# A transformer layer on one core: the four norm vectors brought onto all partitions by DMA instead of by TensorE

## The chip, the cores and the metric

The kernel runs on one core of a Trainium2 chip. The metric is device time in microseconds of a whole execution; less is better. The core's engines are named as in the profile: PE is TensorE's matmul side, PEld its weight loads, DVE is VectorE, ACT is ScalarE, POOL is GpSimd, SP is SyncE, which here only issues DMAs. Each engine works its own list of instructions in order and waits on semaphores for the others.

## The reference

One layer on 512 tokens of width 2048, all in float32: an input projection, three token mixers, an output projection, a first norm, a mixture of experts, a second norm. What matters here is the last part:

```python
x = layer_norm(DEEPNORM_ALPHA * x + mix, ln1_g[l], ln1_b[l])
ffn = hierarchical_moe(x, ...)      # 32 experts, 2 per token; each row is weighted by its gate
x = layer_norm(DEEPNORM_ALPHA * x + ffn, ln2_g[l], ln2_b[l])
# layer_norm(x, g, b) = (x - mu) * rsqrt(var + 1e-5) * g + b, over the 2048 columns
```

`DEEPNORM_ALPHA` is 2 ** 0.25. The gains and offsets `ln1_g`, `ln1_b`, `ln2_g`, `ln2_b` are vectors of 2048 numbers (8 KB). Tokens lie on the 128 partitions, so each vector has to stand on every partition, as a tile of 128 x 2048 (1 MB), before an engine can multiply it into token rows.

## The kernel before

All matrix products are made of three float32r products each (`mm3`, lines 138 to 141): the high parts, and high by low both ways. So each weight chunk of 128 x 1024 float32 (512 KB) is first split into two parts, the high one by ACT (line 85), the low one by DVE (line 86). `Ring` does this for the whole stream of chunks in a fixed order: SP loads a chunk as soon as a raw buffer is free (line 74), ACT and DVE split it when a pair of split buffers is free, PE uses it and gives the pair back (`done`). The raw buffers are filled far ahead of the splits. All weight DMAs leave from SP's one queue, in the order of the program.

The experts are a loop over `e` = 0 to 31. `up(e)` takes 16 chunks, makes the gate and up products of expert e, and ends with the product of the two on DVE (line 1362, tile `B`, once per expert: a good mark of the loop's pace). Behind it `down(e - 1)` takes 8 chunks and makes the rows of the expert before, which POOL adds to the DRAM accumulators `yd` by indirect DMAs (`scatter`, line 1310). POOL also gathers the token rows of expert e + 2 (`gather`, line 1295). The order of every engine's instructions is the order in which the code writes them.

Between `up(e)` and `down(e - 1)` the loop has a place for side work. With e = 12 and e = 21 SP loads two vectors each (`ln1_g` and `ln1_b`, then `ln2_g` and `ln2_b`) onto one partition of tiles `X7` and `B2` (line 1508). With e = 13 and e = 22 `spread` brings them onto all partitions: PE multiplies a row of ones with 512 columns of the vector (line 1344, four times for each tile, in plain float32), and ACT copies the product from PSUM back over the tile (line 1345), for the first norm with ALPHA as its scale. With e = 13 to 20 POOL multiplies half of a token block `z[b]` by `gb1[0]` and adds `gb1[1]` (lines 1515 and 1516), so that behind expert 20 `z` holds ALPHA times the first norm's result. The code that follows the loop adds the experts' sums to `z` and makes the second norm from `gb1` as loaded with e = 21, with EPS in `root` and `refine`.

The weight of an expert's row, `gate`, is made before the loop from `gval` and `w0`; line 1245 is the step of it that the change touches.

Of the kernel before, what the change touches and what calls it, by code (L numbers as in the profile page):

```python
# [20 lines left out]
P = 128  # L21
# [6 lines left out]
# order of the experts: one of each group in turn, so that a token's experts never lie in the same four  # L28
# [3 lines left out]
ALPHA = 2.0 ** 0.25  # L32
SCALE = 192 ** -0.5
# [11 lines left out]
class Ring:  # L45
    """Weight chunks of [128, 1024] float32, loaded ahead and split exactly into two float32r parts."""

    def __init__(self, nc, chunks, beside):
        # beside: chunks of column tiles [k, 64] whose two parts lie next to each other by tiles
        self.nc, self.chunks, self.beside = nc, chunks, beside  # L50
        self.raw, self.hl = [], []
        self.raw_of, self.hl_of = {}, {}
        self.raw_free, self.hl_free = [], []
        self.n_dma = self.n_split = self.n_use = 0
# [63 lines left out]
def _build(tc, nc, ctx, I, out):  # L118
# [28 lines left out]
    # ---------------------------------------------------------------- weight stream  # L147
# [14 lines left out]
    def carver(t):  # L162
        """Parts of a tile, one after another."""
        used = [0]

        def carve(*shape):
            n = int(np.prod(shape))
            v = t[:, used[0]:used[0] + n]
            used[0] += n
            assert used[0] <= t.shape[1]  # L170
            if len(shape) > 1:
                names = "abc"[:len(shape)]
                v = v.rearrange(f"p ({' '.join(names)}) -> p {' '.join(names)}", **dict(zip(names, shape)))
            return v
        return carve

    # what is of no use behind the attention
# [4 lines left out]
    def warm(o, n):  # L182
        """Products that keep TensorE's clock up where it has to wait."""
        for _ in range(n):
            mm(o[:, 0:256], still[:, 0:P], still, start=True, stop=True)

    # ---------------------------------------------------------------- x, split
# [23 lines left out]
    # ---------------------------------------------------------------- constants  # L211
# [19 lines left out]
    eps_c = const("eps_c", [P, 1])  # L231
# [7 lines left out]
    # the first chunk's parts in turn with those of x  # L239
# [9 lines left out]
    # small inputs  # L249
# [21 lines left out]
    # lower bounds: softmax over the layers, cumulative, less the first layer's  # L271
# [13 lines left out]
    # ---------------------------------------------------------------- phase A: x @ w_in  # L285
# [69 lines left out]
    def rotary():  # L355
        for _ in range(5):
            yield
        tt(wsT, wsT, causal[:, None, :].to_broadcast([P, 4, P]), op=OP.mult)
        # rotary tables, by tokens
        posf = early(NB)  # L360
        nc.vector.tensor_copy(posf, posi)
        ang = ftmp[:, 0:128].rearrange("p (b d) -> p b d", b=NB)
        kk_ = ftmp[:, 128:256].rearrange("p (b d) -> p b d", b=NB)
        for b in range(NB):
            ts(ang[:, b, :], invf, posf[:, b:b + 1], None, op0=OP.mult)
        ts(kk_, ang, 1.0 / (2.0 * np.pi), None, op0=OP.mult)
        ts(kk_, kk_, 12582912.0, None, op0=OP.add)
        ts(kk_, kk_, 12582912.0, None, op0=OP.subtract)
        for c in TWO_PI:
            stt(ang, kk_, -c, ang, op0=OP.mult, op1=OP.add)  # L370
        ts(kk_, ang, PI, -PI, op0=OP.min, op1=OP.max)
        act(sinT, kk_, AF.Sin)
        ts(kk_, ang, np.pi / 2, None, op0=OP.is_gt)
        ts(ang, ang, np.pi / 2, None, op0=OP.add)
        stt(ang, kk_, -2.0 * np.pi, ang, op0=OP.mult, op1=OP.add)
        ts(ang, ang, PI, -PI, op0=OP.min, op1=OP.max)
        act(cosT, ang, AF.Sin)
        yield
# [60 lines left out]
    def hgrn():  # L439
# [55 lines left out]
        # the levels of 2 and 1 in one product of S and D: by fours, S holds the keys (to 1 | to itself) of 0, 1 | 2,  # L495
        # D the queries (from itself | from 1 | from 2) of 1 | 2, 3 | 3, the last one in the place of 0
# [105 lines left out]
    # latent q and kv: tiles, and their means of squares  # L602
# [78 lines left out]
    # spatial gating  # L681
# [49 lines left out]
    # ---------------------------------------------------------------- phase B: latent attention  # L731
    V = [(slot(f"X{2 * i}", [NB, 512], F32R), slot(f"X{2 * i + 1}", [NB, 512], F32R)) for i in range(2)]
    # a head's rotary query: its two parts on the halves of the partitions
# [66 lines left out]
    # transposed probabilities: key blocks 0 | 1, 3 | 2, each with the query blocks from its own on  # L800
# [59 lines left out]
    # the experts' rows, added up by tokens; the halves of their columns  # L860
# [40 lines left out]
    # ---------------------------------------------------------------- phase C: output projection, first norm  # L901
# [43 lines left out]
    # the other half of misc: what the weights of the experts take over  # L945
# [10 lines left out]
    def router():  # L956
        for _ in range(4):
            yield
        # rows of the first norm: (z - mu) r g + b, so its products with W are r (z W' - mu c1) + c0, W' = g W
        tt(wt, wg, gcol[:, 1, :, None].to_broadcast([P, KD, 36]), op=OP.mult)  # L960
        s = brt2
        nc.vector.tensor_reduce(s[:, 0:36], wt.rearrange("p k e -> p e k"), axis=AX.X, op=OP.add)
        tt(wg, wg, gcol[:, 0, :, None].to_broadcast([P, KD, 36]), op=OP.mult)
        nc.vector.tensor_reduce(s[:, 36:72], wg.rearrange("p k e -> p e k"), axis=AX.X, op=OP.add)
        split(wgs[:, :, 0], wgs[:, :, 1], wg[:, 0:KT])
        nc.vector.tensor_copy(wg2, wg[:, KT:])
        yield
        o = aux()
        mm(o[:, 0:72], ones, s, start=True, stop=True)
        tt(c0, o[:, 0:36], brt, op=OP.add)  # L970
        nc.vector.tensor_copy(c1, o[:, 36:72])
        lent.extend(ring.add([gb1[0][:, i * 1024:(i + 1) * 1024] for i in range(2)]))
        yield
# [70 lines left out]
    # last columns by token blocks, each block's norm behind them  # L1044
    x1d = dp.tile([T, DM], F32, name="x1d")

    # a block's last columns, statistics, norm (its gain and offset come behind the gather), and routing
# [14 lines left out]
    def centre(b):  # L1062
        """Logits of a block but for the scale and the offset."""
# [7 lines left out]
    def stats(b, o):  # L1071
# [14 lines left out]
        # one more step on r  # L1086
# [11 lines left out]
    def first(dst, src, m, f, n):  # L1098
        """One-hot of the first of the largest entries of src [P, n]; m: the largest."""
# [10 lines left out]
    def route(b):  # L1110
        """Group and two experts of it, of a block's tokens."""
# [53 lines left out]
    # room for the experts' weights  # L1165
# [11 lines left out]
    # one-hot tables of each expert's tokens  # L1177
# [21 lines left out]
    def ranks():  # L1199
        """The tables' part of all blocks but the last."""  # L1200
# [44 lines left out]
    ts(w0, e1, 1.0, None, op0=OP.add)  # L1245
# [26 lines left out]
    # ---------------------------------------------------------------- phase D: experts  # L1272
# [6 lines left out]
    def sized(e, move):  # L1279
        """move(n), n the least of SIZES that holds the expert's first 128 rows."""  # L1280
# [12 lines left out]
    def gather(e):  # L1293
# [8 lines left out]
        else:  # L1302
            # not behind the branches: all else waits for it
# [23 lines left out]
    def rows(e, i, *by):  # L1327
        """Transposes of 4 tiles of an expert's rows, with the first norm's gain and offset."""
# [9 lines left out]

    def spread(t, scale):
        """A row of an input on every partition."""  # L1340
        for n in range(4):
            s = slice(n * 512, (n + 1) * 512)
            o = acc()
            mm(o, ones[0:1, :], t[0:1, s], start=True, stop=True)
            act(t[:, s], o, AF.Copy, scale=scale)  # L1345
# [48 lines left out]
    def steps_of(e):  # L1394
        """Hooks that turn an expert's rows into xT behind the last use of what it holds."""
# [6 lines left out]
    def late():  # L1402
        """Rows of experts with more than 128 tokens: their 128 rows at a time."""
# [70 lines left out]
    for e in range(NE):  # L1474
# [30 lines left out]
        if e in (12, 21):  # L1505
            gb1 = [slot("X7", [DM]), slot("B2", [DM])]
            for t, name in zip(gb1, ("ln1_g", "ln1_b") if e == 12 else ("ln2_g", "ln2_b")):
                nc.sync.dma_start(t[0:1, :], I[name])
        if e in (13, 22):
            for t in gb1:  # L1510
                spread(t, ALPHA if e == 13 else 1.0)
# [17 lines left out]
    # ---------------------------------------------------------------- combination, second norm  # L1529
    Q = [slice(i * 512, (i + 1) * 512) for i in range(4)]  # L1530
    ys = [[slot(t, [DM]) for t in ts] for ts in (("M0", "B3"), ("B4", "X1"), ("B7", "X2"), ("X6", "X3"))]
    # the third behind the last rows of the second half
# [11 lines left out]
    def root(b):  # L1544
        """(variance + EPS) ** -0.5 from ScalarE."""
        r = rs[:, b:b + 1]
        act(r, col(b, 9), AF.Ln, scale=1.0 / DM, bias=eps_c)
        act(r, r, AF.Exp, scale=-0.5)

    def refine(b):  # L1550
        """One more step on it, and the offset; a generator, an instruction at a time."""
        r, v, t = rs[:, b:b + 1], col(b, 10), col(b, 11)
        ts(v, col(b, 9), 1.0 / DM, EPS, op0=OP.mult, op1=OP.add)
# [42 lines left out]
    def run(*seq):  # L1596
        """Instructions of generators woven between the others."""
# [58 lines left out]
def _rows(w, n):  # L1656
    """[k, n] to chunks over column tiles of n: [tiles, 128, k // 128, n]."""
# [67 lines left out]
```

## Time and profile before

| what | value |
|---|---|
| runs (3) | 1997.35, 2002.77, 2004.91 us; median 2002.77 |
| span of the profiled execution | 2000.5 us |
| PE busy, whole span | 1908.9 us (95%) |
| DVE busy, whole span | 1563.6 us (78%) |
| ACT busy, whole span | 1388.8 us (69%) |
| POOL busy, whole span | 408.4 us (20%) |
| moved by DMA, mean | 506.24 MB, 253 GB/s |

The profiled execution is known by its span; its 2000.5 us lie 2.3 us under the median of the runs and inside their spread, so what lies around the span is not more than a few microseconds. Rows below give start, duration, engine, source line, operation and tiles. A busy PE is not a PE at its peak, since matmuls are pipelined and their ends are modelled: the pace is read from starts.

### The profile page before, as it was taken

The page shows a single profiled execution, that of the slowest core. Times are in us where ns is not written, and L with a number is a line of the kernel's source. Part 1 is how long each engine was busy: PE and PEld are TensorE (multiplying, and loading weights), DVE is VectorE, ACT ScalarE, POOL GpSimd, SP SyncE. Part 2 cuts the span into 40 slices and gives each one's busy share as a digit, 9 for nine tenths or more (in the row PEclk, how much of TensorE's full clock was granted, in tenths as well). Part 3 has the DMA queues.
Part 4 walks back from the last instruction along what each step waited for, and adds up shares of the span by engine and source line. Part 5 has one row for each costly group of instructions (what it writes and reads, how often), then busy time and mean ns, then how long its engine had stood idle before and what let it go on. Part 6 is the DMA issues. An engine that isn't in the chain of part 4 may idle for free.

```text
span 2000.5 us, 26829 instructions
## 1 busy us (share of the span) xinstructions
PE 1908.9 (95%) x9067; PEld 1565.0 (78%) x9068; DVE 1563.6 (78%) x2090; ACT 1388.8 (69%) x1844; POOL 408.4 (20%) x216
## 2 busy tenths in 40 slices
PE   9999999999999996999999999999999999999990
PEld 7888888878788895888888888677777878888870
DVE  5666332666564467899999999799999979999987
ACT  3633363645442236899999999788888979999973
POOL 1000000020000012323223241325323214232123
PEclk9999999999999997999999999899999989999995
DMA  6222222341173227899999999799999979999883
GB/s 252 96 74 85 75 77 93 99 142 64 43 270 109 91 107 263 321 360 393 369 386 367 346 366 374 248 364 350 341 355 354 374 289 364 370 379 376 302 290 145
DMA packets 139356, 506.24 MB, mean 253 GB/s; under 512 B 17604, under 2 KB 17652, under 8 KB 137140
## 3 DMA queue, kind: packets, MB, share of 16 engines
q1 hardware_dynamic: 130040, 472.47, 63.8%
q0 software_dynamic: 8576, 30.26, 5.9%
q8 instruction: 72, 1.18, 0.2%
q10 hardware_dynamic: 576, 1.57, 0.2%
q14 instruction: 92, 0.75, 0.1%
HBM read 484.37 MB, written 22.02 MB: 253 GB/s over the span
## 4 chain that ended last, share of the span: by engine, by line
PE 58%; issue 27%; POOL 6%; DMA 4%; DVE 4%; POOLq 1%; ACT 0%; another core or an unknown queue 0%; ACTq 0%; DVEq 0%
PE acc L139 17%; PE acc L140 17%; PE acc L141 17%; DMA yd<-M,idx 3%; POOL yd L1310 2%; PE aux L1320 1%; POOL B L1300 1%; POOL B L1515 1%; PE aux L474 1%; POOL M L1300 1%; DMA B<-x1d,idx 1%; PE acc L839 1%; DVE B L1573 0%; POOL M L1295 0%; PE acc L840 0%
## 5 line engine op out<-in xcount | busy, mean ns | idle before, releaser
L141 PE MATMUL acc<-whl,B 128*128 128x512 f32 (+1 forms) x1368 | 530.5, 388 | 0.3 <-DVE B L145 0.3
L139 PE MATMUL acc<-whl,B 128*128 128x512 f32 (+1 forms) x1312 | 521.9, 398 | 0.0
L140 PE MATMUL acc<-whl,B 128*128 128x512 f32 (+1 forms) x1312 | 512.5, 391 | 4.7 <-DVE whl L86 4.7
L86 DVE TENSOR_TENSOR whl<-X,whl 128x1024 fp32r<-128x1024 f32 x368 | 459.4, 1267 | 68.3 <-ACT whl L85 65.3
L85 ACT ACTIVATE whl<-X 128x1024 fp32r<-128x1024 f32 x368 | 383.1, 1055 | 81.1 <-PE acc L141 74.7
L86 DVE TENSOR_TENSOR whl<-wraw,whl 128x1024 fp32r<-128x1024 f32 (+1 forms) x223 | 275.0, 1245 | 205.1 <-ACT whl L85 198.4
L85 ACT ACTIVATE whl<-wraw 128x1024 fp32r<-128x1024 f32 (+1 forms) x223 | 232.4, 1052 | 222.7 <-PE acc L140 94.7
L1310 POOL DMA_INDIRECT yd<-M,idx x64 | 171.8, 2685 | 774.0 <-ACT M L1385 774.0
L141 PEld LDWEIGHTS acc<-whl,B 128*128 128x128 f32 x1368 | 258.4, 189 | 53.6 <-DVE B L145 0.9
L140 PEld LDWEIGHTS acc<-whl,B 128*128 128x128 f32 x1312 | 248.2, 189 | 58.1 <-DVE whl L86 11.0
L139 PEld LDWEIGHTS acc<-whl,B 128*128 128x128 f32 x1312 | 248.0, 189 | 50.8 <-ACT B L1345 3.0
L139 PE MATMUL acc<-X,B 128*128 128x512 f32 (+1 forms) x432 | 172.2, 399 | 0.0
L141 PE MATMUL acc<-X,B 128*128 128x512 f32 (+1 forms) x440 | 168.9, 384 | 0.0
L140 PE MATMUL acc<-X,B 128*128 128x512 f32 (+1 forms) x432 | 166.7, 386 | 0.8
L86 DVE TENSOR_TENSOR X<-X,X 128x1024 fp32r<-128x1024 f32 x124 | 151.4, 1221 | 18.5 <-ACT X L85 17.8
L139 PE MATMUL acc<-X,whl 128*128 128x512 f32 x384 | 151.1, 394 | 0.7 <-ACT X L144 0.7
L85 ACT ACTIVATE X<-X 128x1024 fp32r<-128x1024 f32 x124 | 131.4, 1059 | 28.6 <-PE acc L141 22.8
L140 PE MATMUL acc<-X,whl 128*128 128x512 f32 x384 | 149.9, 390 | 0.3 <-DVE X L145 0.3
L141 PE MATMUL acc<-X,whl 128*128 128x512 f32 x384 | 149.8, 390 | 0.0
L1385 ACT ACTIVATE M<-acc,X 128x512 f32<-128x512 f32 x128 | 88.3, 690 | 24.9 <-PE acc L141 13.0
L141 PEld LDWEIGHTS acc<-X,B 128*128 128x128 f32 x440 | 83.1, 189 | 16.5
L140 PEld LDWEIGHTS acc<-X,B 128*128 128x128 f32 x432 | 82.0, 190 | 17.3 <-DVE X L86 3.8
(443 smaller groups left out, 3065.3 us busy)
## 6 DMA issues: line engine op xcount, KB each, us to landing
X<-w_up SPq DMA_DIRECT2D x165, 512.0 KB, 5.6
X<-w_gate SPq DMA_DIRECT2D x157, 512.0 KB, 7.3
X<-w_down SPq DMA_DIRECT2D x156, 512.0 KB, 6.8
wraw<-w_gate SPq DMA_DIRECT2D x65, 512.0 KB, 6.9
wraw<-w_in SPq DMA_DIRECT2D x64, 512.0 KB, 3.5
wraw<-w_down SPq DMA_DIRECT2D x60, 512.0 KB, 7.6
wraw<-w_up SPq DMA_DIRECT2D x51, 512.0 KB, 6.2
B<-w_up SPq DMA_DIRECT2D x27, 512.0 KB, 6.0
```

The lines of the kernel that those rows point to most:

```text
L85: nc.scalar.activation(h[:, s], r[:, s], AF.Copy)
L86: nc.vector.tensor_tensor(l[:, s], r[:, s], h[:, s].bitcast(F32), op=OP.subtract)
L139: mm(o, a[0], b[0], start=start, stop=False)
L140: mm(o, a[0], b[1], start=False, stop=False)
L141: mm(o, a[1], b[0], start=False, stop=stop)
L474: mm(ov[r, j], fl(D)[:, c * P:c * P + r.stop], Dv[:, c, :, 1, :], start=True, stop=True)
L839: mm(o[:, :w], qr[h][0:64, qs], kr[1][0:64, :w], start=False, stop=False)
L1300: nc.gpsimd.memset(xgs[e % 2], 0.0)
L1310: nc.gpsimd.indirect_dma_start(out=yd[i][:], out_offset=off(index), in_=y[:, H[i]], in_offset=None, bounds_check=T - 1, oob_is_err=False, ...
L1320: nc.tensor.transpose(o[:, j * P:(j + 1) * P], src[:, k * P:(k + 1) * P], ident)
L1385: act(yts[-1][:, n * 512:(n + 1) * 512], o, AF.Copy, scale=gt[:, EX[e]:EX[e] + 1])
L1515: nc.gpsimd.tensor_tensor(z[b][:, s], z[b][:, s], gb1[0][:, s], op=OP.mult)
```

## The change

`spread` and its two calls go. The loads of line 1508 read the same 8 KB for every partition (`bcast`, a source with a step of 0 from partition to partition) and so fill the 1 MB tiles themselves. Nothing scales `ln1_g` and `ln1_b` by ALPHA any more: `z` is the first norm's result, the gates are divided by ALPHA (line 1245), and the second norm's EPS becomes EPS / ALPHA ** 2, which gives the same result, since a norm does not see the scale of its input but for EPS. A constant column `eps2_c` is added. The rest of the diff takes out comments, which moves line numbers by one to eight.

```diff
+EPS2 = EPS / ALPHA ** 2
...
-    eps_c = const("eps_c", [P, 1])
+    eps_c, eps2_c = const("eps_c", [P, 1]), const("eps2_c", [P, 1])
...
+    nc.vector.memset(eps2_c, EPS2)
...
-    ts(w0, e1, 1.0, None, op0=OP.add)
+    ts(w0, e1, 1.0, ALPHA, op0=OP.add, op1=OP.mult)
...
-    def spread(t, scale):
-        """A row of an input on every partition."""
-        for n in range(4):
-            s = slice(n * 512, (n + 1) * 512)
-            o = acc()
-            mm(o, ones[0:1, :], t[0:1, s], start=True, stop=True)
-            act(t[:, s], o, AF.Copy, scale=scale)
...
             for t, name in zip(gb1, ("ln1_g", "ln1_b") if e == 12 else ("ln2_g", "ln2_b")):
-                nc.sync.dma_start(t[0:1, :], I[name])
-        if e in (13, 22):
-            for t in gb1:
-                spread(t, ALPHA if e == 13 else 1.0)
+                nc.sync.dma_start(t, bcast(I[name], DM))
...
-        act(r, col(b, 9), AF.Ln, scale=1.0 / DM, bias=eps_c)
+        act(r, col(b, 9), AF.Ln, scale=1.0 / DM, bias=eps2_c)
...
-        ts(v, col(b, 9), 1.0 / DM, EPS, op0=OP.mult, op1=OP.add)
+        ts(v, col(b, 9), 1.0 / DM, EPS2, op0=OP.mult, op1=OP.add)
```

On PE, between the last product of `up(13)` and the first of `down(12)`, before (each `mm3` is the lines 139, 140, 141; `B_111` holds the turned rows of expert 12):

```order
L141 MATMUL acc<-whl,B_116_6108 128x512
L1344 MATMUL acc<-X_119_10755,onesr 128x512 x4
L1344 MATMUL acc<-B_120_10756,onesr 128x512 x4
L139 MATMUL acc<-whl,B_111_5464 128x512
L140 MATMUL acc<-whl,B_111_5464 128x512
L141 MATMUL acc<-whl,B_111_5464 128x512
```

And of the change, where the same three lines are 141, 142 and 143:

```order
L142 MATMUL acc<-whl,B_115_6109 128x512
L143 MATMUL acc<-whl,B_116_6110 128x512
L141 MATMUL acc<-whl,B_111_5466 128x512
L142 MATMUL acc<-whl,B_111_5466 128x512
L143 MATMUL acc<-whl,B_111_5466 128x512
```

The eight products of `spread` are gone and nothing stands in their place; ACT's eight copies of line 1345 behind `up(13)` are gone in the same way, and both again behind `up(22)`.

On SP, in the weight stream around `up(12)`, before, with the semaphores that each DMA waits for (DMAHW0 to DMAHW7 are used in turn, so a DMA waits until the eighth before it has landed; DVE is the split that frees the buffer):

```order
L74 DMA R_3990<-w_up 128x1024 [waits DMAHW6_49,DVE_49]
L1508 DMA X_119_10755<-ln_g 1x2048 [waits DMAHW7_49]
L1508 DMA B_120_10756<-ln_b 1x2048 [waits DMAHW0_49]
L74 DMA X_117_6404<-w_up 128x1024 [waits DMAHW1_49,DVE_49]
...
L74 DMA wraw<-w_down 128x1024 [waits DMAHW7_49,DVE_49]
L74 DMA X_97_3980<-w_down 128x1024 [waits DMAHW0_49,DVE_49]
```

And of the change:

```order
L76 DMA R_3992<-w_up 128x1024 [waits DMAHW6_49,DVE_49]
L1503 DMA X_119_10757<-ln_g 128x2048 [waits DMAHW7_49]
L1503 DMA B_120_10758<-ln_b 128x2048 [waits DMAHW0_49]
L76 DMA X_117_6406<-w_up 128x1024 [waits DMAHW1_49,DVE_49]
...
L76 DMA wraw<-w_down 128x1024 [waits DMAHW7_49,DVE_49]
L76 DMA X_97_3982<-w_down 128x1024 [waits DMAHW0_49,DVE_49]
```

The place is the same; the two DMAs move 128 rows where they moved one, and the weight DMAs that wait for DMAHW7 and DMAHW0 behind them now wait for the landing of 1 MB each.

On POOL, the first multiply and add on `z` behind the gather for expert 15 (`B_109`), before:

```order
L1295 DMA B_109_5385<-x1d,idx 16x2048 [waits Pool_49]
L1287 UNCONDITIONAL_BRANCH
L1515 TENSOR_TENSOR B_92_3971<-B_92_3971,X_119_10755 128x1024 [waits DMAHW7_49,Activation_49]
L1516 TENSOR_TENSOR B_92_3971<-B_92_3971,B_120_10756 128x1024 [waits DMAHW0_49,Activation_49,Pool_49]
L1281 TENSOR_LOAD cnt_i
```

And of the change:

```order
L1298 DMA B_109_5387<-x1d,idx 16x2048 [waits Pool_49]
L1290 UNCONDITIONAL_BRANCH
L1507 TENSOR_TENSOR B_92_3973<-B_92_3973,X_119_10757 128x1024 [waits DMAHW7_49]
L1508 TENSOR_TENSOR B_92_3973<-B_92_3973,B_120_10758 128x1024 [waits DMAHW0_49,Pool_49]
L1284 TENSOR_LOAD cnt_i
```

The order on POOL is the same, but these two no longer wait for ACT, which copied the spread products, only for the loads.

## Rows read from the trace of the kernel before

**Rows 1.** Three stretches: busy time by engine, granted clock, DMA share, GB/s
```profile
core 0: us, PE busy (x) PEld busy (x) DVE busy (x) ACT busy (x) POOL busy (x), PEclk, DMA share, GB/s
1217.40:1252.40 35.00, 35.00 (x161) 28.17 (x160) 33.84 (x39) 32.41 (x43) 9.99 (x4) 1.00 1.00 376
...
1262.20:1267.30 5.10, 5.10 (x14) 3.98 (x14) 1.05 (x1) 1.65 (x2) 0.00 (x0) 0.53 0.00 0
1304.10:1341.70 37.60, 36.12 (x165) 28.62 (x164) 37.29 (x40) 32.72 (x42) 12.68 (x6) 1.00 1.01 360
```

**Rows 2.** Timeline of DVE, the row of line 1362 of six experts
```profile
1217.35 0.68 DVE L1362 TENSOR_TENSOR B<-B,acc 128x512 f32<-128x512 f32 x1
...
1252.43 0.69 DVE L1362 TENSOR_TENSOR B<-B,acc 128x512 f32<-128x512 f32 x1
...
1304.10 0.68 DVE L1362 TENSOR_TENSOR B<-B,acc 128x512 f32<-128x512 f32 x1
...
1341.70 0.68 DVE L1362 TENSOR_TENSOR B<-B,acc 128x512 f32<-128x512 f32 x1
...
1599.65 0.68 DVE L1362 TENSOR_TENSOR B<-B,acc 128x512 f32<-128x512 f32 x1
...
1646.95 0.68 DVE L1362 TENSOR_TENSOR B<-B,acc 128x512 f32<-128x512 f32 x1
```

**Rows 3.** Timeline of PE around the first spread
```profile
1250.44 0.39 PE L141 MATMUL acc<-whl,B 128*128 128x512 f32 x1
1250.76 4.67 PE L1344 MATMUL acc<-X,onesr 1*128 1x512 f32 x8
1255.23 7.03 PE L1344 MATMUL acc<-B,onesr 1*128 1x512 f32 x8
1262.19 0.80 PE L139 MATMUL acc<-whl,B 128*128 128x512 f32 x1
```

**Rows 4.** Timeline of POOL: a gather, then the first two multiplies, one add
```profile
1231.81 2.01 POOL L1295 DMA_INDIRECT B<-x1d,idx  x1 [0.30 <-POOL B L1300]
1253.50 3.56 POOL L1515 TENSOR_TENSOR B<-B,X 128x1024 f32<-128x1024 f32 x1 [19.68 <-ACT X L1345]
...
1282.81 2.50 POOL L1515 TENSOR_TENSOR B<-B,X 128x1024 f32<-128x1024 f32 x1
1285.39 3.27 POOL L1516 TENSOR_TENSOR B<-B,B 128x1024 f32<-128x1024 f32 x1
```

**Rows 5.** Timeline of DVE beside and behind those POOL rows
```profile
1283.62 6.13 DVE L86 TENSOR_TENSOR whl<-X,whl 128x1024 fp32r<-128x1024 f32 x2
...
1293.22 2.34 DVE L86 TENSOR_TENSOR whl<-wraw,whl 128x1024 fp32r<-128x1024 f32 x2
```

**Rows 6.** One raw buffer, R: SP's load, its landing, ACT's read; then a vector's load
```profile
1219.20 0.33 SPq L74 DMA_DIRECT2D R<-w_up  x1
1219.58 0.33 SPq L1508 DMA_DIRECT2D X<-ln_g  x1
...
1241.41 1.05 ACT L85 ACTIVATE whl<-R 128x1024 fp32r<-128x1024 f32 x1
...
R<-w_up SPq DMA_DIRECT2D x1, 512.0 KB, 4.9
```

**Rows 7.** Waits of SP from 1060 to 1240 us: total, times, longest
```profile
SPq L74 <- DVE whl L86: 96.7, 88, 3.9
```

**Rows 8.** DMAs of the first 40 us: size, us to landing; two of their issues
```profile
B<-ws_T POOLq DMA_DIRECT2D x1, 256.0 KB, 6.6
B<-sgu_ln_g POOLq DMA_DIRECT2D x1, 256.0 KB, 7.4
B<-sgu_ln_b POOLq DMA_DIRECT2D x1, 256.0 KB, 8.3
B<-sgu_b POOLq DMA_DIRECT2D x1, 256.0 KB, 10.0
...
5.54 0.54 POOL L253 DMA_DIRECT2D B<-ws_T  x1
...
7.12 0.54 POOL L253 DMA_DIRECT2D B<-sgu_b  x1
```

## Prediction

> **What bounds the kernel now.** I read the busy shares in the table first, then the pace of the expert loop, then the stretch around the edited lines, and last how much room the weight stream has.
>
> In an ordinary expert, the first row of [rows 1], PE is busy for all 35.00 us at full granted clock, DVE for 33.84 us, and the DMA share is 1.00 at 376 GB/s. Three resources look full at once, so the question is which one sets the pace. The mark on DVE once per expert [rows 2] has three distances. From 1217.35 to 1252.43 it is 35.08 us: the pace with nothing beside it. From 1304.10 to 1341.70 it is 37.60 us: an expert with a multiply and an add on POOL. There PE is busy for only 36.12 of 37.60 us while DVE is at 37.29 (the last row of [rows 1]), so DVE sets that pace. The third kind holds the spreads: 51.67 us from 1252.43 to 1304.10, and 47.30 us from 1599.65 to 1646.95.
>
> What happens in them is in [rows 3]. The last expert matmul starts at 1250.44 and the next one at 1262.19. The 11.75 us between belong to the spread's products: 4.67 us for the tile X7 and 7.03 us for B2. PE is the engine that all others wait for there, so this is time on the path, not work in its shade. After it PE's clock is low: 1.2 GHz instead of 2.4, a granted clock of 0.53 from 1262.20 to 1267.30 (the second row of [rows 1]), right behind the spread's products.
>
> **What goes.** The second spread costs 47.30 - 35.08 = 12.22 us whole, with its clock loss. The first cannot be read off in the same way, since an expert with POOL work lies in its distance: 51.67 - 37.60 = 14.07 us. As a cross-check from its parts: 11.75 us of gap, and half-rate work, 5.1 x (1 - 0.53) = 2.4 us; 14.15 us, less the one matmul step that lies in the gap anyway. The two ways agree within 0.3 us. So 14.07 + 12.22 = 26.29 us go. ACT's sixteen copies go too; they lie inside these stretches and are not counted again.
>
> **What comes onto the path: the first POOL work.** This is the term that the diff hides. In the kernel before, the first multiply on `z` waits 19.68 us for the spread and starts at 1253.50 [rows 4], inside the stall; it was free, since 35.08 + 14.15 + 2.52 for the next pair at 1282.81 (priced below) already make 51.75 of the 51.67 us. Now it waits only for the loads. The chunk just ahead of the loads took 4.9 us to land [rows 6]; two loads of 1.05 MB at the 376 GB/s of the stretch add 2.8 us each, so both have landed at about 1219.58 + 4.9 + 5.6 = 1230.1. The gather ahead of the multiply on POOL ends at 1231.81 + 2.01 = 1233.8 [rows 4]. So it starts there, some 20 us earlier, in the middle of `up(13)` at full pace. What that does is in [rows 5]: while POOL works 2.50 + 3.27 us on the next half block, two splits on DVE take 6.13 us, where two take 2.34 us without it. DVE loses 3.8 us, and it has 35.00 - 33.84 = 1.2 us of room in an expert. The rest, 2.6 us, is what the pace shows: 37.60 - 35.08 = 2.52 us. I take 2.52; the bounds are 0 (split pairs made ahead cover it) and 3.8 us (no room helps). The seven later POOL pairs cost what they cost before.
>
> **What the loads themselves cost.** Each of two places puts 2.10 MB into the weight stream instead of 16 KB. The trace has no such load at full stream, so I bound it. By the stream's rate they take 5.6 us at each place. By the slowest neighbours: at the start of the kernel three vectors of 2 KB are spread over the partitions in the same way, 256 KB each, issued right behind an ordinary load of 256 KB. That one landed at 5.54 + 6.6 = 12.1, the last vector at 7.12 + 10.0 = 17.1 [rows 8]: 5.0 us for three, 1.66 us for 256 KB while weights also came in, which makes 6.6 us for 1 MB and 13.3 us for two. Cover: the chunk issued at 1219.20 landed after 4.9 us and was read by ACT at 1241.41 [rows 6], so it lay ready for 22.2 - 4.9 = 17.3 us. A delay of 5.6 to 13.3 us in the chunks behind is within that, and costs nothing. SP itself may wait: the seventh and eighth weight DMAs behind the loads wait for these loads' landings, and all later weights are queued behind them. The same 17.3 us cover that wait. With the cover gone, each microsecond of delay would be one of PE's. And the stream can win the room back, since what SP waits for in steady state is the split that frees a buffer (96.7 us in 180, 88 times [rows 7]), not a landing; in the eight experts with POOL work it also has 2.5 us more time for the same bytes.
>
> The other edits: one more memset of one column on DVE at the start, and a second scalar operation in an instruction on 128 x 4 numbers that stands there anyway; constants in `root` and `refine`. Under 0.2 us together; I count zero.
>
> **Sum.** 2000.5 - 26.29 + 2.52 = 1976.7 us of span. The median of the runs lies 2.3 us above the span of the profiled execution; I keep that distance: **1979.0 us**, a ratio of 0.988.
>
> **Rivals.**
>
> *The DMA engines are the true limit.* Their share is 1.00 in the ordinary expert [rows 1]. If the pace of 35.08 us were theirs as well as PE's, the stream could not make up for 2 x 2.08 MB more, and 4.16 MB at 376 GB/s, 11.1 us, would come back: 1979.0 + 11.1 = 1990.1 us. Against it: SP waits for buffers, chunks lie ready for 17 us, and DMA had nothing to move from 1262.20 to 1267.30 [rows 1] because all buffers were full after a stall. For a part of it: the two places may each lose a few of the 5.6 us where gathers and scatters share the engines.
>
> *One row read 128 times is slow.* All 128 partitions read the same 8 KB of HBM, and this could serialize at one place in memory. Let T be the time that both loads hold up the stream; each place then loses T - 17.3 us. It decides from 2 x (T - 17.3) = 23.8, so T = 29.2 us, 72 GB/s for 2.10 MB. If the slowest vector's 10.0 us from issue to landing [rows 8] grew in proportion to its bytes, T would be 40 us, the loss 22.7 us at each place, and the time 1979.0 + 45.4 = 2024.4 us: slower than before. Against it: the three vectors of the start came at 786 KB in 5.0 us, 157 GB/s, twice the threshold, while sharing the engines with the weights; and they read 2 KB rows, four times shorter. The Trainium skill has a figure that speaks for this rival (SBUF — State Buffer, in the part on a bandwidth-pool intuition): HBM is reached over 32 ports of some 22.5 GB/s each. By it, as an estimate from that page, a row behind one port would take 47 us for 1 MB; the small vectors of this trace came faster than that already, but whether an 8 KB row lies behind more than one port no row here shows.
>
> *The first POOL work stays free.* If the pairs split ahead cover DVE's 3.8 us, 2.52 us are saved: 1976.5 us. In the seven experts that show it, nothing covered it.
>
> *The change does not do what it says.* That the products are gone is in the order of the instructions; nothing takes their place on PE.
>
> **How the numbers follow.** The main forecast, 1979.0 us, has 0.78; its own range is 1974 to 1984, from the bounds of the POOL term (1976.5 to 1980.3) and the spread of the runs, 3 us either way. The first POOL work free: 0.07. A DMA limit in whole or part, 1984 to 1992: 0.10. The slow row: 0.05. The range 1971 to 1990 holds the first two and most of the third. Half a percent, about what a measurement of this kernel can tell from no change, is 10 us: faster means under 1992.8. The slow row's 0.05 spreads over all outcomes above; I give 0.03 of it to slower and 0.02, with 0.02 of the DMA case, to the same: 0.93, 0.04, 0.03.
>
> **What would show it.** In the profile after: no gap between the last matmul of `up(13)` and the next; granted clock 1.00 there; marks of line 1362 at 37.6 us for expert 13 to 14, at 37.6 for the one that had 51.67, and at 35.08 for the one that had 47.30. The first multiply on POOL would start near 1234, and the vectors' loads would land within some 8 to 20 us of their issue. ACT would wait for no weight DMA. I am wrong if ACT's splits wait for DMAs behind the loads, if the loads take 30 us or more, or if the distance for expert 13 to 14 is far from 37.6.

## The result and the profile after

The changed kernel takes 1986.39 us, the median of 7 runs (1983.13 to 1994.39), against 2004.91 us of the kernel before (7 runs, 1997.35 to 2005.72): a ratio of 0.992 with a 95% interval of 0.990 to 0.9939. It is faster, and inside the range of the prediction, but 7.4 us above the predicted 1979.0. The profiled execution took 1983.13 us with a span of 1981.3, so 19.2 us of span are gone where 23.8 were forecast.

Three stretches of the changed kernel: span from and to, length, then busy time by engine, PE's granted clock, DMA share and GB/s. They answer to [rows 1].

```profile
core 0: us, PE busy (x) PEld busy (x) DVE busy (x) ACT busy (x) POOL busy (x), PEclk, DMA share, GB/s
1216.50:1255.20 38.70, 36.90 (x169) 29.25 (x167) 38.33 (x39) 33.53 (x43) 16.86 (x6) 1.00 1.01 387
1255.30:1293.90 38.60, 36.11 (x164) 28.60 (x164) 38.28 (x39) 32.74 (x42) 13.66 (x6) 1.00 0.95 342
1628.70:1663.70 35.00, 35.00 (x165) 29.01 (x164) 33.92 (x39) 32.52 (x43) 11.23 (x4) 1.00 1.03 392
```

The first stretch holds the first place's loads, the second one replaces the stall. The granted clock is 1.00 in both, and the DMAs never stop. The first place's 38.7 us with DVE busy for 38.33 of them is already the odd thing: an expert with POOL work was to take 37.6.

The mark on DVE once per expert, as in [rows 2]; its line is now 1357:

```profile
1216.47 0.68 DVE L1357 TENSOR_TENSOR B<-B,acc 128x512 f32<-128x512 f32 x1
1255.27 0.67 DVE L1357 TENSOR_TENSOR B<-B,acc 128x512 f32<-128x512 f32 x1
1293.93 0.68 DVE L1357 TENSOR_TENSOR B<-B,acc 128x512 f32<-128x512 f32 x1
1331.54 0.68 DVE L1357 TENSOR_TENSOR B<-B,acc 128x512 f32<-128x512 f32 x1
...
1593.70 0.68 DVE L1357 TENSOR_TENSOR B<-B,acc 128x512 f32<-128x512 f32 x1
1628.71 0.68 DVE L1357 TENSOR_TENSOR B<-B,acc 128x512 f32<-128x512 f32 x1
```

The first distance is 38.80 us (35.08 before, 37.60 forecast), the second 38.66 (51.67 before, 37.60 forecast), the third 37.61, and where the second spread lay it is 35.01 (47.30 before, 35.08 forecast). The five further POOL experts, not shown, have 38.64, 38.65, 38.63, 37.60 and 38.71. So the two stalls are gone whole, and the experts with POOL work now come in two kinds: two of eight at the known 37.6 us, six at 38.6 to 38.8.

PE at the end of `up(13)`, where [rows 3] had 11.75 us of spread products:

```profile
1254.91 0.39 PE L143 MATMUL acc<-X,B 128*128 128x512 f32 x1
1255.99 0.66 PE L1323 MATMUL aux<-identr,B 128*128 128x128 f32 x4 [0.70 <-DVE B L1357]
```

What is left is 0.70 us in which PE waits for a late DVE. POOL in three experts, each with a gather, then the multiply and the add (as in [rows 4]):

```profile
1230.88 3.15 POOL L1298 DMA_INDIRECT B<-x1d,idx  x1 [0.30 <-POOL B L1303]
1234.07 2.41 POOL L1507 TENSOR_TENSOR B<-B,X 128x1024 f32<-128x1024 f32 x1
1236.55 3.27 POOL L1508 TENSOR_TENSOR B<-B,B 128x1024 f32<-128x1024 f32 x1
...
1269.70 3.01 POOL L1298 DMA_INDIRECT M<-x1d,idx  x1 [0.30 <-POOL M L1303]
1272.73 2.42 POOL L1507 TENSOR_TENSOR B<-B,X 128x1024 f32<-128x1024 f32 x1
1275.23 3.25 POOL L1508 TENSOR_TENSOR B<-B,B 128x1024 f32<-128x1024 f32 x1
...
1308.31 1.92 POOL L1298 DMA_INDIRECT B<-x1d,idx  x1 [0.27 <-POOL B L1303]
1310.26 2.48 POOL L1507 TENSOR_TENSOR B<-B,X 128x1024 f32<-128x1024 f32 x1
1312.83 3.27 POOL L1508 TENSOR_TENSOR B<-B,B 128x1024 f32<-128x1024 f32 x1
```

The first multiply starts at 1234.07, directly behind its gather: the vectors were there. The pairs themselves are alike. What differs is the gather ahead of them, 3.0 to 3.15 us in the two slow experts and 1.92 in the third. DVE's splits beside the second and the third of these, as in [rows 5]:

```profile
1270.62 1.22 DVE L88 TENSOR_TENSOR whl<-X,whl 128x1024 fp32r<-128x1024 f32 x1
...
1272.39 7.17 DVE L88 TENSOR_TENSOR whl<-X,whl 128x1024 fp32r<-128x1024 f32 x2
...
1309.27 1.22 DVE L88 TENSOR_TENSOR whl<-X,whl 128x1024 fp32r<-128x1024 f32 x1
...
1311.05 6.13 DVE L88 TENSOR_TENSOR whl<-X,whl 128x1024 fp32r<-128x1024 f32 x2
```

Read the ends. With the long gather, the multiply starts 0.34 us after the two splits' start (1272.73 against 1272.39), the add ends at 1278.48, the second split at 1279.56. With the short one, the multiply starts 0.79 us before the splits (1310.26 against 1311.05), while DVE ends the split before (1309.27 + 1.22) and then makes small scalings; the add ends at 1316.10, the second split at 1317.18. Both times the split ends 1.08 us behind the add, and so it is in all eight experts (1.07 to 1.09). DVE gets free when POOL's pair is over, so a pair that starts 1.1 us later against the splits costs DVE 7.17 - 6.13 = 1.04 us more. POOL waits as well: the add takes 3.25 to 3.27 us here, but 2.34 us inside the stall of the kernel before, where DVE ran nothing:

```profile
1259.62 2.34 POOL L1516 TENSOR_TENSOR B<-B,B 128x1024 f32<-128x1024 f32 x1 [2.55 <-issue]
```

The Trainium skill (SBUF — State Buffer, "SBUF: two separate sides") says that a VectorE operation with two SBUF inputs and a GpSimd operation that reads SBUF take a shared port pair as an exclusive lock for a whole instruction. The trace agrees in the ends; it does not show that whichever starts first wins, since the split that started 0.34 us ahead of the multiply still ended 1.1 us behind it.

The sizes close. DVE's loss against the undisturbed 2.34 us is 3.79 us with the short gather and 4.83 with the long one; against this kernel's plain distance of 35.03 the pace loses 37.60 - 35.03 = 2.57 and 38.65 - 35.03 = 3.62. The difference, what the expert hides, is 1.2 us both times.

### The profile page after: what moved, and what is told of

It reads as the page before. It is cut to its first block, busy times and chain, and to the rows that moved or that the text cites. A ratio compares the mean times of both kernels' runs of the same rounds, so it can differ in the third digit from the quotient of the medians.

```text
span 1981.3 us, 26745 instructions
## 1 busy us (share of the span) xinstructions
PE 1884.6 (95%) x9035; PEld 1554.8 (78%) x9036; DVE 1572.9 (79%) x2091; ACT 1380.0 (70%) x1828; POOL 428.2 (22%) x216
## 4 chain that ended last, share of the span: by engine, by line
issue 43%; PE 35%; POOL 8%; DMA 8%; DVE 4%; POOLq 1%; ACT 1%; another core or an unknown queue 0%; ACTq 0%; DVEq 0%
PE acc L141 10%; PE acc L142 10%; PE acc L143 10%; DMA yd<-M,idx 7%; POOL yd L1313 4%; POOL B L1303 1%; POOL M L1303 1%; POOL B L1507 1%; PE aux L477 1%; POOL M L1298 1%; DMA B<-x1d,idx 1%; POOL B L1298 1%; PE acc L842 1%; POOLq L1284 0%; DVE B L1565 0%
## 5 line engine op out<-in xcount | busy, mean ns | idle before, releaser
L88 DVE TENSOR_TENSOR whl<-X,whl 128x1024 fp32r<-128x1024 f32 x368 | 466.5, 1286 | 45.8 <-ACT whl L87 42.7
L87 ACT ACTIVATE X<-X 128x1024 fp32r<-128x1024 f32 x124 | 131.4, 1060 | 28.7 <-PE acc L143 23.0
```

Of the source, the lines that this page charges most:

```text
L87: nc.scalar.activation(h[:, s], r[:, s], AF.Copy)
L88: nc.vector.tensor_tensor(l[:, s], r[:, s], h[:, s].bitcast(F32), op=OP.subtract)
```

## The experiments

The theory behind the result: the spreads were PE's time and went whole, the loads are free, and the shortfall is the phase of the pairs, that is, where among DVE's splits a pair starts. The rivals: the loads slow the splits down, or the stream is full and gives the time back elsewhere. Each of e1 to e8 is a single run, so they are read by the distances in their profiles first. Experiments e1 to e4 ran beside a run of the kernel before of 2006.27 us, e5 to e8 beside one of 2008.19.

**e1 and e2: both kernels once more, no edit.**

> The kernel before, unchanged, for a second profile. Theory A (a race): after's POOL pairs mostly cost 3.6 us of pace where before's cost 2.5, because the gather ahead of them ends 1.1 us later when it misses the gap between two splits on DVE, and which way that falls is not fixed by the code: here some of the seven experts with POOL work take 38.6 us instead of 37.6, or gathers' lengths of 1.9 and 3.1 us are dealt out otherwise than in the first profile. Theory B (the change does it): all seven at 37.6 us again, gathers in that stage all 1.9 to 2.0 us. Both: span 1995 to 2005 us.

> The changed kernel, unchanged, for a second profile. Theory A (a race): the eight experts with POOL work again take either 37.6 or 38.7 us, but in another pattern and number than six of eight. Theory B (the change does it): six or more of eight at 38.6 to 38.8 us, in the same places. Both: span 1979 to 1992 us, no gap behind up(13) and up(22).

Measured: 2003.18 us (span 2001.1) and 1984.51 us (span 1982.7). The mark of the kernel before, behind the first spread:

```profile
1303.72 0.68 DVE L1362 TENSOR_TENSOR B<-B,acc 128x512 f32<-128x512 f32 x1
1342.40 0.67 DVE L1362 TENSOR_TENSOR B<-B,acc 128x512 f32<-128x512 f32 x1
1379.99 0.68 DVE L1362 TENSOR_TENSOR B<-B,acc 128x512 f32<-128x512 f32 x1
```

And of the changed kernel, at the first place:

```profile
1215.88 0.68 DVE L1357 TENSOR_TENSOR B<-B,acc 128x512 f32<-128x512 f32 x1
1253.67 0.67 DVE L1357 TENSOR_TENSOR B<-B,acc 128x512 f32<-128x512 f32 x1
1292.34 0.67 DVE L1357 TENSOR_TENSOR B<-B,acc 128x512 f32<-128x512 f32 x1
```

In the kernel before, one distance is 38.68 us this time and the next 37.59, with a 3.05 us gather in the slow one: the slow kind is not a property of the change. In the changed kernel six of eight are slow again, but others: the first expert, which moves the 2 MB of loads, has 37.79 us here and had 38.80 in the first profile. So the loads do not make the slow kind. When these loads landed is recorded in e2's profile (the one after has no landing of them):

```profile
X<-ln_g SPq DMA_DIRECT2D x1, 1024.0 KB, 7.2
B<-ln_b SPq DMA_DIRECT2D x1, 1024.0 KB, 10.5
```

**e3: the change at the second place alone** (an edit of the kernel before).

```diff
-                nc.sync.dma_start(t[0:1, :], I[name])
-        if e in (13, 22):
+                nc.sync.dma_start(*((t[0:1, :], I[name]) if e == 12 else (t, bcast(I[name], DM))))
+        if e == 13:
...
-                spread(t, ALPHA if e == 13 else 1.0)
+                spread(t, ALPHA)
```

> Only ln2_g and ln2_b come by DMA; ln1 is spread by TensorE as before, with ALPHA in it. My theory: the distance that held 47.30 us falls to 35.0 to 35.1, the one with the first spread stays at 51.7 (or 52.7 where the gather ends late), span 12.2 us under that of before at the same lengths of its POOL experts: about 1988 us if those are 37.6, up to 1996 if all are 38.6. Rival (2 MB in the stream cost something): the 47.30 falls to 38 us or more, or the experts behind it run over 35.1 us.

Measured: 1991.88 us, span 1990.1. The mark at the second place:

```profile
1601.73 0.68 DVE L1362 TENSOR_TENSOR B<-B,acc 128x512 f32<-128x512 f32 x1
1636.76 0.68 DVE L1362 TENSOR_TENSOR B<-B,acc 128x512 f32<-128x512 f32 x1
```

35.03 us where 47.30 was: 12.27 us gone there, forecast 12.22. The first spread still costs 51.64 us, and every later POOL expert takes 37.6.

**e5: the change at the first place alone** (an edit of the changed kernel: the products of `spread` kept behind `up(22)`, the function `spread` put back).

```diff
...
-                nc.sync.dma_start(t, bcast(I[name], DM))
+                nc.sync.dma_start(*((t, bcast(I[name], DM)) if e == 12 else (t[0:1, :], I[name])))
+        if e == 22:
+            for t in gb1:
+                spread(t, 1.0)
```

> Only ln1_g and ln1_b come by DMA; ln2 is spread by TensorE as before. My theory: the distance from expert 13 to 14 that held 51.67 us becomes 37.6 or 38.7, the one before it (12 to 13) rises from 35.1 to 37.8 or 38.8 since the first POOL pair now lies in it, the one with the second spread stays at 47.3. Span 12.2 us over the changed kernel's: 1993 to 1995 us. Rival (the later gather is a matter of the second place, or of the whole program): POOL experts at 37.6 us throughout here.

Measured: 1996.64 us, span 1994.9. The mark at the first place is at 1216.26, 1255.04 and 1293.71 (38.78 and 38.67 us), seven of eight POOL experts are of the slow kind, and the second spread keeps its cost:

```profile
1594.54 0.68 DVE L1364 TENSOR_TENSOR B<-B,acc 128x512 f32<-128x512 f32 x1
1641.75 0.68 DVE L1364 TENSOR_TENSOR B<-B,acc 128x512 f32<-128x512 f32 x1
```

Seven of eight are of the slow kind here, none of seven in e3. This is not the first place's edit alone: e5 also has the rest of the change (gates, EPS2, the column `eps2_c`), e3 has none of it, and the two programs differ before either place is reached. In experts 1 to 11 the gather is long (over 3 us) 9 times in e5, 8 times in the changed kernel, 6 in e2 and 9 in e4, but 5 times in e3, 4 in the kernel before and 2 in e1.

**e4: four more 1 MB copies of each vector, into scratch memory in DRAM that nothing reads.** 8.4 MB more at each place, on top of the 2.1.

```diff
+    extra = [dp.tile([4, P, DM], F32, name=f"extra{i}") for i in range(4)]
...
                 nc.sync.dma_start(t, bcast(I[name], DM))
+                for x in extra:
+                    nc.sync.dma_start(x[e // 20 * 2 + (t is gb1[1])], bcast(I[name], DM))
```

> The changed kernel with each of the four vectors' loads followed by four more of the same 1 MB, into DRAM scratch that nothing reads: 10.5 MB at each place instead of 2.1. Theory (17.3 us of cover in the stream, loads at the stream's rate): some 28 us of loads, so PE loses about 28 - 17 = 11 us at each place, span about 2003 us, and ACT's splits wait for weight DMAs there. Rival 1 (the DMA engines are the limit already): every extra byte costs, 16.8 MB at 376 GB/s, 45 us, span about 2026 us. Rival 2 (one row read by all partitions is slow in bulk): over 2040 us.

Measured: 2015.61 us, span 2013.8. DMAs of 1215 to 1260 us (size, median us to landing):

```profile
extra<-ln_g SPq DMA_DIRECT2D x4, 1024.0 KB, 16.2
extra<-ln_b SPq DMA_DIRECT2D x4, 1024.0 KB, 25.3
...
X<-ln_g SPq DMA_DIRECT2D x1, 1024.0 KB, 7.9
```

Waits of 1215 to 1275 us (total, times, longest):

```profile
ACT X L87 <- DMA X<-w_up: 15.3, 1, 15.3
...
PEld acc L141 <- ACT X L87: 12.2, 1, 12.2
```

The stretch behind, with the columns of the table of stretches above:

```profile
1248.00:1268.00 20.00, 7.74 (x23) 5.60 (x22) 7.97 (x9) 7.95 (x10) 0.79 (x1) 0.66 1.01 377
```

Here the cover is used up: ACT waits once for a weight chunk, 15.3 us at the first place and 17.2 at the second, and the clock falls to 0.66 behind it. As an estimate, 10.5 MB at the 362 GB/s of 1215 to 1260 us are 29 us, and 29 less the 12 to 14 us that PE waited leaves 15 to 17 us of cover, near the 17.3 of [rows 6]. The span was expected near 2003 and is 11 us above it: the two places cost 12.2 and 16.8 us against the changed kernel, where 11 each were forecast, a sum that had left out the low clock; some 3 us lie elsewhere. It is 12 us under the 2026 of the DMA limit, so the time alone does not choose between the two; e6 does. In the changed kernel, with a fifth of these bytes, ACT never waited for such a chunk.

**e6: no multiply and add on `z`** (both lines of POOL's work taken out).

> The changed kernel without POOL's multiply and add on z (the first norm's gain and offset are left out of the residual). My theory, that the pairs cost what the distances 12 to 20 of the changed kernel show over 35.03 us (307.3 - 280.2 = 27.1 us): span 1981.3 - 27.1 = 1954 us, all distances 35.0. Rival (part of these 27 us is the 2 MB of loads): the distances 12 to 14 stay above 35.1 and the span above 1956 us.

Measured: 1956.17 us, span 1954.4. All distances are 35.0 to 35.1 us, those at the first place too, which holds the same loads:

```profile
1216.39 0.68 DVE L1357 TENSOR_TENSOR B<-B,acc 128x512 f32<-128x512 f32 x1
1251.42 0.68 DVE L1357 TENSOR_TENSOR B<-B,acc 128x512 f32<-128x512 f32 x1
1286.45 0.68 DVE L1357 TENSOR_TENSOR B<-B,acc 128x512 f32<-128x512 f32 x1
```

Gathers of both lengths are among them: the long gather costs nothing by itself. Adding the changed kernel's eight excesses over 35.03, 27.1 us together, gives 1954.4 + 27.1 = 1981.5 us, against its span of 1981.3. The POOL pairs are the whole difference.

**e7: the pair ahead of the gather on POOL**, one expert later, so that the gather's length cannot shift it.

```diff
-        if 13 <= e < 21:
+        if 14 <= e < 22:
...
```

(the indices follow, and the block moves to where it is issued before the next gather)

> The changed kernel with each POOL pair ahead of the gather instead of right behind it (and one expert later in the loop's text, so that it follows the scatter). If the 1.05 us between 37.6 and 38.65 come from a gather that ends late and lets the pair start inside a split: all eight distances come out alike here, whatever the gathers' lengths, at 37.6 if the pair meets no split at its start and near 38.7 if it does. If they come from something else in the program (DMA, buffers): the mix of both stays. Span 1978 to 1983 us.

Measured: 1993.85 us, span 1992.1. All eight POOL experts are alike, as expected, but dear: 39.2 to 39.4 us. DVE's two splits:

```profile
1264.47 4.48 DVE L88 TENSOR_TENSOR whl<-X,whl 128x1024 fp32r<-128x1024 f32 x1 [0.36 <-ACT whl L87]
1268.88 3.39 DVE L88 TENSOR_TENSOR whl<-B,whl 128x1024 fp32r<-128x1024 f32 x1
```

POOL's pair beside them:

```profile
1264.94 2.92 POOL L1473 TENSOR_TENSOR B<-B,X 128x1024 f32<-128x1024 f32 x1
1267.94 3.25 POOL L1474 TENSOR_TENSOR B<-B,B 128x1024 f32<-128x1024 f32 x1
```

The pair starts 0.47 us behind the splits' start, the worst phase yet; the second split ends at 1272.27, 1.08 us behind the add's 1271.19. DVE loses 7.80 - 2.34 = 5.46 us, the pace of the eight 39.26 - 35.03 = 4.23 on average: again 1.2 hidden. That all eight are alike was expected, but neither of the two prices expected (37.6 and 38.7) came, and the span is 9 us over the expected one. Against the long-gather kind DVE loses 0.63 us more: 0.13 by the later start, 0.50 because the pair itself takes 6.25 us instead of 5.75 (the multiply 2.92 for 2.42), which nothing here explains.

**e8: the pair on DVE** (`nc.gpsimd.tensor_tensor` becomes `tt`).

> The changed kernel with the multiply and the add on z made by DVE itself instead of POOL. My theory (the pair costs DVE's time while POOL holds it up, not POOL's work): two operations of 1.22 us less 1.17 us of room, 1.27 us an expert, eight times 10 us in place of 27: span 1964 us, distances 36.3. Rival (any work put beside the splits costs its full length, since DVE has no usable room): 2.44 an expert, span 1974 us. Rival (the pace of these experts is set by something else than DVE): 1981 us.

Measured: 1978.53 us, span 1976.8. A POOL expert becomes one of 36.97 us, 1.94 more than a plain one, for two operations of 1.22 and 1.23 us; 1.27 was expected, 2.44 by the rival, and it came out between. Only 0.5 us of the lump is hidden here, behind the end of `up`. This run's loop began 5.6 us late (first mark at 810.47 instead of 804.9), with a low clock in a stretch long before the edit. That stretch in this run (busy times, granted clock, DMA share, GB/s as above):

```profile
440.00:470.00 30.00, 28.21 (x122) 22.06 (x120) 19.25 (x34) 16.85 (x33) 0.00 (x0) 0.77 0.43 148
```

And in the changed kernel:

```profile
440.00:470.00 30.00, 28.24 (x150) 22.02 (x149) 24.04 (x48) 19.44 (x41) 0.00 (x0) 1.00 0.53 183
```

DVE and ACT run 34 and 33 instructions in it instead of 48 and 41, so the loop starts later. Why the clock was low there is not shown. Without those 5.6 us the span would be near 1971, by an estimate, where 1964 was expected and 1974 by the rival.

**e9: the pair on DVE in 20 thin pieces**, 410 columns behind each of the experts 11 to 30.

```diff
+        if 11 <= e < 31:
+            b, i = divmod(e - 11, 5)
+            s = slice(i * 410, min(i * 410 + 410, DM))
+            tt(z[b][:, s], z[b][:, s], gb1[0][:, s], op=OP.mult)
+            tt(z[b][:, s], z[b][:, s], gb1[1][:, s], op=OP.add)
-        if e in (12, 21):
+        if e in (10, 30):
...
```

> The multiply and add on z made by DVE in 20 experts, 410 columns in each, instead of 1024 columns in 8; ln1 is loaded with e = 10, ln2 with e = 30. If what costs in the eight experts is that a lump of 2.44 us is larger than DVE's room of 1.17 us and the little work made ahead, two operations of 0.58 us each fit: distances 35.0 to 35.3, span 1955 to 1960 us. Rival (DVE's room cannot be used, work beside the splits costs its length whatever its size): 20 x 1.16 = 23 us over the kernel without the pairs, span 1977 us, as with eight lumps.

Measured: 1970.57 us (4 runs), ratio 0.9836 (0.9814 to 0.9858), beside 2004.36 of the kernel before. The two pieces, and 35.68 us per expert:

```profile
1255.01 0.57 DVE L1503 TENSOR_TENSOR B<-B,X 128x410 f32<-128x410 f32 x1
1255.61 0.59 DVE L1504 TENSOR_TENSOR B<-B,B 128x410 f32<-128x410 f32 x1
```

1.16 us of work cost 35.68 - 35.03 = 0.65: 0.5 hidden once more. This lies between the two expected outcomes as well (35.3 us at most, or the full 1.16 on top); the span of 1968.1 missed the expected 1955 to 1960.

**e10: the offset without an engine.** The rows `yd`, into which the experts' results are added, start from `ln1_b` instead of zeros, written by two broadcast DMAs; DVE only multiplies, 512 columns behind each of 16 experts.

```diff
+    for i, y in enumerate(yd):
+        v = bcast(I["ln1_b"], DM)
+        nc.gpsimd.dma_start(y, bass.AP(tensor=v.tensor, offset=v.offset + i * (DM // 2), ap=[[0, T], [1, DM // 2]]))
...
+        if 11 <= e < 27:
+            b, i = divmod(e - 11, 4)
+            s = slice(i * 512, i * 512 + 512)
+            tt(z[b][:, s], z[b][:, s], gb1[0][:, s], op=OP.mult)
...
```

> A version to beat both: the accumulators yd start from ln1_b on every row (two DMAs inside HBM) in place of zero, so the add on z goes; the multiply by ln1_g is made by DVE, 512 columns in each of 16 experts (0.69 us each, under DVE's room of 1.17); ln1_g is loaded with e = 10, ln2 with e = 27. My theory: all expert distances 35.0 to 35.1, span 1954 to 1956 us, ratio to before 0.977. Rival (the DMAs inside HBM hold up the gated work around 436 us, or the room cannot be used): 11 us or more above, span over 1965 us.

Measured: 1960.07 us (5 runs, 1958.99 to 1966.56), ratio 0.9785 (0.9765 to 0.9806), the fastest complete kernel of the study. The multiply, and two marks:

```profile
1251.59 0.68 DVE L1357 TENSOR_TENSOR B<-B,acc 128x512 f32<-128x512 f32 x1
...
1253.92 0.68 DVE L1503 TENSOR_TENSOR B<-B,X 128x512 f32<-128x512 f32 x1
...
1286.76 0.68 DVE L1357 TENSOR_TENSOR B<-B,acc 128x512 f32<-128x512 f32 x1
```

0.68 us of work costs 35.17 - 35.03 = 0.14 us, so nearly all of it lies in DVE's 0.5 us (35.0 to 35.1 us an expert were expected). The span of 1957.2 is 2.8 us above that of e6, which has none of this work, and 1.2 above the expected 1954 to 1956.

## Why the prediction was right, and where it was off

*The spreads.* -26.29 us were forecast. The second place gave 12.29 (47.30 - 35.01), or 12.27 alone in e3, for 12.22. The first gave 51.67 - 38.66 = 13.01 for 14.07; the missing 1.06 is the slow kind of POOL expert, since the stall and the low clock behind it are gone (granted clock 1.00). The 14.07 is the price in one execution: the clock had fallen inside the products already (granted 0.61 from 1250.70 to 1262.20), and in e1, where it fell later, the gap was 10.55 us instead of 11.75 and the distance 51.03 us, though a long gather lies in it.

*The first POOL pair.* +2.52 us forecast with bounds of 0 and 3.8; it measured 38.80 - 35.08 = 3.72. (The prediction calls this distance "expert 13 to 14"; it runs from the mark of expert 12 to that of 13.) Its place and start were right (1234.07 for "near 1234"). The size was taken from the short-gather experts, the only kind with a pair in that trace; 6 of its 28 gathers from expert 1 on were long (3.06 to 3.20 us), all in experts without a pair. That 3.72 lies inside the bounds is luck: the upper one took DVE's loss for 3.8 with no room, and the loss was 4.84 with 1.1 hidden.

*"The seven later POOL pairs cost what they cost before."* This is the step that failed: a pair's price changed with its phase, from 2.5 to 3.6 us. Counting the expert that had the stall as above, the other six cost 4.2 us more in all, because four of them are of the slow kind. With 1.20 and 1.06 that makes 6.5 us. Some 1.9 us came back elsewhere: plain experts are some 0.04 us shorter each, the first mark comes 0.4 us and the end 0.5 us earlier. 23.8 - 6.5 + 1.9 = 19.2 is the span's gain. The other 2.8 us of the miss are the choice to keep the kernel before's distance of 2.3 us from span to median: the profiled execution was the fastest of seven, and the median lies 5.1 us above its span. What made others up to 11 us longer is not shown; two more experts of the slow kind would be 2.1 us.

*The room on DVE.* The 35.00 - 33.84 = 1.2 us taken for it holds at POOL's place, where 1.2 was hidden for losses of 3.79, 4.83 and 5.46 us. It does not hold elsewhere: behind the end of `up`, e8, e9 and e10 all hid 0.5 to 0.55 us.

*The loads.* Free, as forecast, with cover near 17 us (e4): in e6 the first place runs at 35.03 us. With a pair beside the loads that expert takes 0.13 to 0.18 us more than others of its kind (38.80, 37.79 and 38.78 in after, e2 and e5), for a reason not shown. In e2 the second load landed 11.0 us behind the first one's issue, where 10.5 were forecast, and in the changed kernel SP waited 1.8 us for that landing, which the cover took. The rival of the slow row falls: the two 1 MB broadcasts landed 7.2 and 10.5 us after their issue in e2 (8 to 20 were forecast), and in e4 ten (eight of them into DRAM) went through while the core's DMAs moved 362 GB/s. The Trainium skill's 22.5 GB/s for an HBM port (SBUF — State Buffer, the bandwidth-pool part), by which an estimate gave 47 us for 1 MB if one row lay behind one port, does not describe what happened here.

*The DMA limit.* The median of 1986.39 lies in that rival's stretch of times, and outside the likeliest case's 1974 to 1984, yet its mechanism is not what was at work: no wait of ACT for weights, and e6 runs at 35.0 us per expert with the same loads. So the forecast range held the time through a stretch that it had for another reason, which is luck.

*What stays open.* Why the changed kernel has mostly long gathers. Short or long, a gather ends 0.82 to 0.92 us behind the end of a split in all 19 of the changed kernel's trace from 1125 to 1800 us: the first split's end or the next one's. Which of them goes with some 20 to 30 ns in ACT's part of the second split, which runs into the gather. With the long gather, then the short one:

```profile
1269.46 1.06 ACT L87 ACTIVATE whl<-X 128x1024 fp32r<-128x1024 f32 x1 [0.30 <-PE acc L143]
...
1308.13 1.06 ACT L87 ACTIVATE whl<-X 128x1024 fp32r<-128x1024 f32 x1 [0.33 <-PE acc L143]
```

ACT ends 0.10 us before DVE's second split starts at 1270.62, and 0.08 before the one at 1309.27. Over the 28 gathers of this trace it is 0.09 to 0.11 us with the long ones and 0.07 to 0.08 with the short ones. That is a correlation; nothing here moved those 20 ns alone. The slow kind is commoner in the changed programs (6 of 8, 6 of 8 in e2, 7 of 8 in e5 and e4) than in the others (none of 7, two of 7 in e1, none in e3); that the first place's edit makes it is not shown. Two things go with it. The long gathers are commoner in the changed programs from the loop's start on, by the counts under e5. And they are rare behind a spread: in the six experts 14 to 19 there are none, 1 and none where `spread` ran ahead of them (before, e1, e3) and 4, 5, 5 and 5 where it did not (after, e2, e4, e5); in the experts 23 to 28 there are 2, none and 2 with it (before, e1, e5) and 4, 6, 4 and 6 without it (after, e2, e4, e3). So the stall that the change took away went with the cheap phase; by what path stays open.

## What to carry to other kernels

Beside a DVE that is busy for 33.8 of 35.0 us, the price of the same POOL pair went from 2.6 over 3.6 to 4.2 us with its phase: read where among DVE's operations it starts and which one ends behind it, and do not carry a price over when the change moves what stands ahead of it. A free load may expose work that a stall had hidden, and that work may be cheaper in thin pieces on the busy engine itself (20 x 0.65 = 13 us in e9 for the same work as the 27.1 us of the POOL pairs; 16 x 0.14 = 2.2 us in e10, where the offset comes from a DMA). One expert's idle DVE time is not one pool: measure what hides where.

## What the runs showed of the hardware

A multiply and an add of 128x1024 on POOL, 5.7 to 6.3 us together, took 3.8, 4.8 or 5.5 us from DVE's splits as their start moved from 0.79 us ahead of the splits to 0.34 and 0.47 behind (the last in e7, with a longer multiply). A gather's issue on POOL took 1.9 or 3.1 us beside such splits, ending 0.8 to 0.9 us behind one split or the next; the Trainium skill (SBUF — State Buffer, "SBUF: two separate sides") tells of GpSimd being kept from writing a DMA's descriptors while VectorE runs an operation in a two-port mode, and its bandwidth-pool part gives some 115 ns behind the operation's end for a case of its own. The gathers here end 0.82 to 0.92 us behind a split, and splits are TENSOR_TENSOR operations; whether they are held by the same thing no run here shows. And a row of 8 KB read for 128 partitions, 1 MB, landed in 7.2 us (e2) and 7.9 us (e4) amid a full weight stream.
